# One fused transformer kernel: scan inputs with the next block's products beside them, and attention's key sets joined pair by pair

## Chip, core and metric

The kernel runs on one core of a Trainium2 chip. The metric is the device time in microseconds, the median of repeated runs of the whole program. The engines are named as in the profile: PE (TensorE), DVE (VectorE), ACT (ScalarE), POOL (GpSimd), SP (SyncE); their DMA queues are SPq, ACTq and POOLq.

## What is computed

The program computes two transformer blocks in a row on 512 tokens of width 1024. The first is a hybrid block (dilated window attention, a Mamba-2 scan, gates, SwiGLU); the second has two layers, the first with an RWKV-7 scan in both directions and a spatial gate, the second with an mLSTM. The change touches the attention of the first block and the inputs of the RWKV-7 scan for x in the second.

```python
DILATED_GROUPS = ((128, 1), (512, 4), (2048, 16))    # 3 groups x 8 heads of 64
# attention: each group by itself, with a bias by distance, then a softmax over the groups
logits = einsum(qb, kw) * HEAD_DIM ** -0.5 + bias     # bias (8, 128, 256) per group
m = max(logits); p = exp(logits - m); den = sum(p)
o = einsum(p, vw) / den;  lse = m + log(den)
alpha = softmax(stack(lses)); attn = sum(alpha * o)   # the join
merged = gates[:, :, 0] * (attn @ w_attn_branch) + gates[:, :, 1] * (ssm @ w_ssm_branch)
...
# scan inputs (rwkv_prep), for the context (256 tokens) and for x (512 tokens)
r, k, v = split(dwconv1d(p[..., o:o + 3 * B_WIDTH], b_shift), 3)
logw = -softplus(-(b_w0 + einsum(tanh(wd), b_w_up))) - 0.5;  decay = exp(-exp(logw))
a = sigmoid(b_a0 + einsum(ad, b_a_up))
kk = k * b_kk;  kk = kk * rsqrt(max(sum(kk * kk), 1e-12))
k_dir = k * (1 + (a - 1) * b_ka)
```

## The kernel before

Each float32 matmul against a weight is made of three: `wload` loads 512 KB of weights (`wraw`, by SPq), ACT rounds it to a high part (`whi`, L292), DVE takes the rest (`wlo`, L293), and `mm3` or `tok` issue low x high, high x low and high x high (L301 to L303, L384 to L386). The three tiles have three buffers each. One unit of 512 KB stands for 24 matmuls of 128x512 (L301 to L303 with 8 blocks of rows, or 4 token tiles with 2).

The order of the work is written by hand with generators: `par` takes one step of each in turn, `merge` runs that to the end, and `blend` and `between` hand out steps by a count of matmul columns (`self.work`). A scheduler then lays the instructions out at compile time on each engine, by this order and by when it expects operands and buffers; on the chip every engine and queue works through its list in order.

**Attention.** `rel_bias` makes the bias tables. For each group a matmul gives an 8-partition row table (one per head, 384 or 256 wide), a DVE copy brings it to SBUF, and a POOL DMA writes it to DRAM (`scr`) 128 times in a row; a second POOL DMA reads that back with a row pitch one element shorter, which shifts the row for each partition (`B0`, `B12`). POOL's queue holds these five DMAs in order, and the read of a table stands before the write of the next but one. Meanwhile V is projected (12 units of `w_v`). Then four head pairs `hp` follow: `units` (products, DVE maximum, ACT Exp, transposes, products with V) runs in step with `qk` of the next pair, for the last pair with 5 of 8 gate products (`gates`). There are two key sets: `sid` 0 is group 0, `sid` 1 is groups 1 and 2. Each has its maximum and its denominator in `st` and its output in `Os`.

`attn_join` joins the two sets of all heads at once, when all pairs are done: transpose `st`, write to DRAM (`dstat`), read back with the heads on 8 partitions (`R`), weights by maximum, Exp, sums and reciprocal (8x512 each), write (`dw`), read back on all partitions (`Wb`, 2 DMAs for each pair), and per pair two multiplies, an add and the split to `ah`, `al`. All these DMAs are SP's. The rest of the gates runs beside it. Behind it 8 products with `w_ab` (4 units) read `ah`, `al`.

**Scan inputs.** `mix0_proj` runs three products (blocks 16 to 18), then four blocks `b`. Each block has three products (`block_mm`, r, k, v, 24 matmuls each, a step ends after three rows of blocks), each evacuated by `conv3` in one ACT and two DVE operations; then a chain on DVE, ACT and POOL with six small products (sum of squares L1346; per direction decay L1357 and rate L1362; the bonus L1402 behind the whole chain) and the DMAs that store the scan's inputs. Every product there, and the chain's, takes one of the two PSUM buffers of `psO` (`fps`). It runs for the context (T = 256) beside the first block's FFN, and for x (T = 512, `two` = 2: r, k, v and four chain tiles have two buffers) beside the first steps of the scan itself (`mix0_scan`, L1480 to L1626), with products of `ada_units` (L1017) in between.

Of the kernel before, what the change touches and what calls it, by code (L numbers as in the profile page):

```python
# [249 lines left out]
class Kern:  # L250
# [177 lines left out]
    def rel_bias(self, pool):  # L428
# [6 lines left out]
        tab, es = flat()[:NBUCKET + 1, :896], flat()[:8]  # L435
# [3 lines left out]
        nc.gpsimd.dma_start(lhs[0:NBUCKET], D["relb"])  # L439
        off = 0  # L440
        for g, L in enumerate((384, 256, 256)):
            ps = self.btile()[:8, :L]
            nc.tensor.matmul(ps, lhs[:, g * 8:(g + 1) * 8], tab[:, off:off + L], start=True, stop=True)
            e = es[:, off:off + L]
            off += L
            nc.vector.tensor_copy(e, ps)
            scr = self.dram.tile([8, P * L + 512], F32, name="scr%d" % g)
            dst = scr[:, :P * L].rearrange("h (p l) -> h p l", l=L)
            nc.gpsimd.dma_start(dst, e.unsqueeze(1).to_broadcast([8, P, L]))
            src = scr[:, :P * (L - 1)].rearrange("h (p l) -> p h l", l=L - 1)  # L450
            if g == 0:
                nc.gpsimd.dma_start(B0, src[:, :, 0:256])
            else:
                nc.gpsimd.dma_start(B12[:, :, (g - 1) * P:g * P], src[:, :, 0:P])
        return B0, B12

    def attn_unit(self, pool, hp, sid, half, qT, kT, V, bias, st, O):
# [9 lines left out]
        for u in range(2):  # L467
# [13 lines left out]
            for e in range(2):  # L481
                h = 2 * hp + e
                nc.vector.tensor_tensor_reduce(p[:, e, u, lo:], S[e][:, u, lo:], bias[:, h, lo:], 1.0, -3e38,
                                               op0=ALU.add, op1=ALU.max, accum_out=st[:, 2 * sid, h, i:i + 1])
        mx = st[:, 2 * sid, 2 * hp:2 * hp + 2, 2 * half:2 * half + 2]
        nc.vector.tensor_scalar(ng.rearrange("p (e u) -> p e u", e=2), mx, -1.0, None, op0=ALU.mult)
        for u in range(2):
            i = 2 * half + u
            lo = P if sid == 0 and i == 0 else 0
            for e in range(2):  # L490
                h = 2 * hp + e
                nc.scalar.activation(p[:, e, u, lo:], p[:, e, u, lo:], AF.Exp, bias=ng[:, 2 * e + u:2 * e + u + 1],
                                     accum_out=st[:, 2 * sid + 1, h, i:i + 1])
# [24 lines left out]
    def attention(self, xT, ah, al, other):  # L518
# [3 lines left out]
        with self.tc.tile_pool(name="ao", bufs=1) as op:  # L522
          st = op.tile([P, 4, 8, 4], F32, name="st")
          Os = op.tile([P, 4, 2, SEQ], F32, name="Os")
          with self.tc.tile_pool(name="at", bufs=2) as pool:
# [26 lines left out]
            def units(hp, qT, kT):  # L552

                last = None
                for sid in range(2):
                    O = self.psO.tile([P, SEQ], F32, name="pso")
                    for half in range(2):
                        u = self.attn_unit(pool, hp, sid, half, qT, kT, V, (B0, B12)[sid], st, O)
# [12 lines left out]
            for hp in range(4):  # L571
                merge(units(hp, *qk_[hp]), qk(hp + 1, *qk_[hp + 1]) if hp < 3 else islice(other, 5))
          with self.tc.tile_pool(name="ac", bufs=2) as pool:
              merge(self.attn_join(pool, st, Os, ah, al), other)

    def attn_end(self, last, Os):
        _, hp, sid, half, O = last
        if half:
            self.nc.scalar.copy(Os[:, hp, sid], O)

    def attn_join(self, pool, st, Os, ah, al):

        nc = self.nc
        ps = self.btile()[:, :P]
        nc.tensor.transpose(ps, st.rearrange("p a b c -> p (a b c)"), self.ident)
        sT = pool.tile([P, P], F32, name="sT", bufs=1)
        nc.vector.tensor_copy(sT, ps)
        dst = self.dram.tile([4, 8, 4, P], F32, name="dstat")
        nc.sync.dma_start(dst.rearrange("a b c p -> (a b c) p"), sT)
        R = pool.tile([8, 4, SEQ], F32, name="R", bufs=1)  # L590
        nc.sync.dma_start(R, dst.rearrange("a b c p -> b a (c p)"))
        v = lambda i: R[:, i].rearrange("h (r i) -> h i r", r=4)
        n = lambda t: t.rearrange("h (i r) -> h i r", r=4)
        W = pool.tile([8, 2, SEQ], F32, name="W", bufs=1)
        tm = pool.tile([8, 2, SEQ], F32, name="tm", bufs=1)
        M, L = tm[:, 0], tm[:, 1]
        V_, S_ = nc.vector, nc.scalar
        yield
        V_.tensor_tensor(n(M), n(R[:, 0]), v(2), op=ALU.max)
        V_.tensor_tensor(W[:, 0], R[:, 0], M, op=ALU.subtract)  # L600
        V_.tensor_tensor(n(W[:, 1]), v(2), n(M), op=ALU.subtract)
        S_.activation(W, W, AF.Exp)
        V_.tensor_tensor(L, W[:, 0], R[:, 1], op=ALU.mult)
        V_.tensor_tensor(n(M), n(W[:, 1]), v(3), op=ALU.mult)
        V_.tensor_tensor(L, L, M, op=ALU.add)
        V_.reciprocal(L, L)
        V_.tensor_tensor(W, W, L.unsqueeze(1).to_broadcast([8, 2, SEQ]), op=ALU.mult)
        dw = self.dram.tile([8, 2, SEQ], F32, name="dw")
        nc.sync.dma_start(dw, W)
        yield  # L610
        for hp in range(4):
            Wb = pool.tile([P, 2, SEQ], F32, name="Wb")
            for e in range(2):
                nc.sync.dma_start(Wb[64 * e:64 * e + 64], dw[2 * hp + e].unsqueeze(0).to_broadcast([64, 2, SEQ]))
            y = pool.tile([P, SEQ], F32, name="ay")
            z = pool.tile([P, SEQ], F32, name="az")
            V_.tensor_tensor(y, Os[:, hp, 0], Wb[:, 0], op=ALU.mult)
            V_.tensor_tensor(n(z), Os[:, hp, 1].rearrange("d (r i) -> d i r", r=4), n(Wb[:, 1]), op=ALU.mult)
            V_.tensor_tensor(y, y, z, op=ALU.add)
            self.dump("attnT%d" % hp, y)  # L620
            self.split(ah[:, hp], al[:, hp], y)
            yield
# [229 lines left out]
    def block1_(self, keep, c1):  # L852
# [5 lines left out]
        with tc.tile_pool(name="b1", bufs=1) as pl:  # L858
# [13 lines left out]
            with tc.tile_pool(name="ahl", bufs=1) as ap_:  # L872
# [3 lines left out]
                with tc.tile_pool(name="gp", bufs=1) as gp:  # L876
                    gts = [gp.tile([P, SEQ], F32, name="g%d" % i) for i in range(8)]
                    self.attention(xT, ah, al, self.gates(xT, 0, gts))
                    for s in range(4):
                        w = self.wload(D["w_ab"], s, 1)  # L880
                        for j in range(2):
                            fb = 2 * s + j
                            ps = self.ptile()
                            self.feat(ps, w, 0, (ah, al), kbn=4, off=j * 512)
# [424 lines left out]
    def mix0_proj(self, pool, T, xT, up, io):  # L1309
# [20 lines left out]
        for b in range(4):  # L1330
            rkv = []
# [917 lines left out]
```

## Time and profile before

| | |
|---|---|
| runs | 3446.86, 3434.73, 3446.99 us; median 3446.86 |
| profiled execution, own time | 3435.72 us |
| its span | 3433.8 us, so 1.9 us lie around it |
| PE, DVE, ACT, POOL busy | 93%, 59%, 40%, 7% of the span |
| mean granted clock | 0.972 |

A span is the time from the first to the last instruction of the profiled execution. [...] Matmuls overlap in the pipeline, so the time from one start to the next is the price of one, not its listed duration.

### The profile page before, as it was taken

How to read it: one execution, taken by the hardware profiler on the slowest of the kernel's cores; microseconds unless marked ns; L12 is line 12 of the kernel's file. 1: busy time of each engine (PE TensorE's matmuls, PEld its weight loads, DVE VectorE, ACT ScalarE, POOL GpSimd, SP SyncE). 2: the span in 40 equal slices, each digit the busy share in tenths (PEclk: the TensorE clock that was granted, in tenths of full speed). 3: DMA queues.
4: the chain of work that ended last, by engine and by line, in shares of the span. 5: the costliest groups of instructions: out<-in, count | busy, mean ns of one | idle time of the engine just before them, and what ended most of it. 6: DMA issues, size and time to landing. Idle time of an engine off the chain costs nothing.

```text
span 3433.8 us, 53206 instructions
## 1 busy us (share of the span) xinstructions
PE 3209.5 (93%) x21803; PEld 2567.3 (75%) x21803; DVE 2010.4 (59%) x3226; ACT 1383.1 (40%) x2294; POOL 226.9 (7%) x260
## 2 busy tenths in 40 slices
PE   6999799999889999889899999989999989899998
PEld 5877577777677788766577888767788767778887
DVE  2333567775645543556655656667565754766656
ACT  2233244342344442443344444446532444543323
POOL 0000000000100000022121121000000200000001
PEclk9999999999999999999899999999999989999999
DMA  7411343445444432434555544542322325232323
GB/s 135 128 62 62 109 140 128 135 148 177 148 138 136 128 111 98 139 119 119 151 164 164 169 160 137 177 168 89 108 95 92 133 95 172 89 105 92 98 92 111
DMA packets 216843, 430.96 MB, mean 126 GB/s; under 512 B 75426, under 2 KB 114546, under 8 KB 216344
## 3 DMA queue, kind: packets, MB, share of 16 engines
q1 hardware_dynamic: 193736, 370.09, 34.1%
q10 hardware_dynamic: 20464, 51.58, 4.0%
q0 software_dynamic: 2400, 5.90, 1.7%
q8 instruction: 171, 2.80, 0.3%
q14 instruction: 72, 0.59, 0.1%
HBM read 380.70 MB, written 46.79 MB: 124 GB/s over the span
## 4 chain that ended last, share of the span: by engine, by line
PE 77%; DVE 9%; DMA 7%; ACT 4%; issue 2%; POOL 0%; SPq 0%; ACTq 0%; POOLq 0%; DVEq 0%
PE psa L301 11%; PE psa L303 11%; PE psa L302 11%; PE psa L385 5%; PE psa L384 5%; PE psa L386 5%; PE pso L301 3%; PE pso L303 3%; PE pso L302 3%; DVE wlo L293 2%; DMA wraw<-in_w_v_dram 1%; PE psa L1552 1%; ACT whi L292 1%; PE psa L1562 1%; PE pso L1017 1%
## 5 line engine op out<-in xcount | busy, mean ns | idle before, releaser
L293 DVE TENSOR_TENSOR wlo<-wraw,whi 128x1024 fp32r<-128x1024 f32 x480 | 597.5, 1246 | 524.2 <-ACT whi L292 518.7
L292 ACT CAST whi<-wraw 128x1024 fp32r<-128x1024 f32 x482 | 503.7, 1046 | 773.0 <-PE psa L386 224.6
L301 PE MATMUL psa<-xh,wlo 128*128 128x512 f32 (+1 forms) x1760 | 693.3, 396 | 18.0 <-DVE wlo L293 10.7
L303 PE MATMUL psa<-xh,whi 128*128 128x512 f32 (+1 forms) x1760 | 684.7, 390 | 0.0
L302 PE MATMUL psa<-xl,whi 128*128 128x512 f32 (+1 forms) x1760 | 683.7, 389 | 0.0
L301 PEld LDWEIGHTS psa<-xh,wlo 128*128 128x128 f32 x1760 | 335.6, 192 | 97.6 <-DVE wlo L293 14.9
L303 PEld LDWEIGHTS psa<-xh,whi 128*128 128x128 f32 x1760 | 336.0, 191 | 72.7 <-issue 4.2
L302 PEld LDWEIGHTS psa<-xl,whi 128*128 128x128 f32 x1760 | 336.3, 191 | 71.6 <-issue 3.8
L1138 DVE SCALAR_TENSOR_TENSOR fc<-psa,f_cv,fc 128x441 f32<-128x441 f32 (+2 forms) x352 | 243.4, 692 | 41.4 <-ACT fc L1127 34.5
L301 PE MATMUL pso<-xh,wlo 128*128 128x256 f32 (+1 forms) x720 | 232.0, 322 | 0.6 <-ACT u L1445 0.5
L302 PE MATMUL pso<-xl,whi 128*128 128x256 f32 (+1 forms) x720 | 222.0, 308 | 1.0 <-DVE xl L347 1.0
L303 PE MATMUL pso<-xh,whi 128*128 128x256 f32 (+1 forms) x720 | 221.8, 308 | 0.0
L385 PE MATMUL psa<-wlo,ah 128*128 128x512 f32 x528 | 210.9, 399 | 2.8 <-DVE wlo L293 2.5
L384 PE MATMUL psa<-whi,al 128*128 128x512 f32 x528 | 209.0, 399 | 3.4 <-ACT whi L292 3.4
L386 PE MATMUL psa<-whi,ah 128*128 128x512 f32 x528 | 209.7, 398 | 0.0
L301 PEld LDWEIGHTS pso<-xh,wlo 128*128 128x128 f32 x720 | 137.0, 190 | 12.9 <-issue 1.7
L302 PEld LDWEIGHTS pso<-xl,whi 128*128 128x128 f32 x720 | 136.9, 190 | 9.6 <-DVE xl L347 1.6
L303 PEld LDWEIGHTS pso<-xh,whi 128*128 128x128 f32 x720 | 136.5, 190 | 8.2 <-issue 0.8
L384 PE MATMUL psa<-whi,xl 128*128 128x512 f32 x288 | 117.6, 410 | 19.3 <-ACT whi L292 16.0
L385 PEld LDWEIGHTS psa<-wlo,ah 128*128 128x128 f32 x528 | 99.0, 188 | 30.1 <-DVE wlo L293 6.3
L384 PEld LDWEIGHTS psa<-whi,al 128*128 128x128 f32 x528 | 98.8, 187 | 29.6 <-ACT whi L292 4.7
L385 PE MATMUL psa<-wlo,xh 128*128 128x512 f32 x288 | 117.2, 407 | 1.1 <-DVE wlo L293 1.1
(554 smaller groups left out, 5168.5 us busy)
## 6 DMA issues: line engine op xcount, KB each, us to landing
wraw<-in_f_up_dram SPq DMA_DIRECT2D x132, 512.0 KB, 3.8
wraw<-in_ada_w_dram SPq DMA_DIRECT2D x96, 512.0 KB, 3.6
wraw<-in_f_dn_dram SPq DMA_DIRECT2D x66, 512.0 KB, 3.5
wraw<-in_w_fi_dram SPq DMA_DIRECT2D x44, 512.0 KB, 3.5
wraw<-in_ab_f_dram SPq DMA_DIRECT2D x38, 512.0 KB, 3.8
wraw<-in_w_qk_dram SPq DMA_DIRECT2D x24, 512.0 KB, 3.7
wraw<-in_w_xbc_dram SPq DMA_DIRECT2D x24, 512.0 KB, 4.7
wraw<-in_c_f_dram SPq DMA_DIRECT2D x24, 512.0 KB, 4.3
```

The source lines that it names most:

```text
L292: nc.scalar.copy(hi, raw)
L293: (eng or nc.vector).tensor_tensor(lo, raw, hi.bitcast(F32), op=ALU.subtract)
L301: mm(ps, wl, xh, start=start, stop=False)
L302: mm(ps, wh, xl, start=False, stop=False)
L303: mm(ps, wh, xh, start=False, stop=stop)
L384: mm(ps, sl, wh[:, c], start=first and k == 0, stop=False)
L385: mm(ps, sh, wl[:, c], start=False, stop=False)
L386: mm(ps, sh, wh[:, c], start=False, stop=last and k == kbn - 1)
L1017: nc.tensor.matmul(ps[o:o + 32], self.cs[:, 4 * h + j, 22 - 2 * i:54 - 2 * i], raw[:, j * 256:(j + 1) * 256], start=h == 0, stop=h == 1, t ...
L1138: V_.scalar_tensor_tensor(o, pv[:, r0 + dr:r1 + dr, c0 + dc:c1 + dc], cw(i), o, op0=ALU.mult, op1=ALU.add)
L1552: mm(ps[h, d, b], Al[h, d, b], Tm[h, d, b], start=True, stop=True, tile_position=(64 * e, 64 * e))
L1562: mm(ps[h, d, b], lt[h, d, b], rt[h, d, b], start=True, stop=True, tile_position=(64 * e, 64 * e))
```

## The change

1. `rel_bias`: the 24 columns of the bias table are repeated 16 times on the free side (`rep`), so that the matmul gives each head's row on 16 partitions, 128 in all. The DRAM write then takes 8 copies from each of 128 partitions, in place of 128 copies from each of 8.
2. Attention: `st` and `Os` are kept by pair. `attn_join` does one pair, as a generator of five steps; the join of a pair runs beside the next pair's units, that of the last beside the remaining gates, of which there are 4 in place of 3. R has the pair's two heads and four row groups on 8 partitions, so that its operations are 8x128. The DMAs move from SP to ACT (5 per pair, `dstat`) and POOL (R, `dw`, two `Wb`).
3. Products with `w_ab`: 4 outputs at a time, first with the rows of the first three pairs for all four, then with those of the last pair.
4. `mix0_proj`: `blocks` (the three products) and `chain` are split; for x, the chain of block b takes turns with the products of block b + 1. For the context the order stays.

```diff
@@ -432,21 +432,24 @@
         B12 = pool.tile([P, 8, 256], F32, name="B12", bufs=1)
 
         flat = lambda: pool.tile([P, 2, 2, 256], F32, name="p").rearrange("p a b c -> p (a b c)")
-        tab, es = flat()[:NBUCKET + 1, :896], flat()[:8]
+        tab, es = flat()[:NBUCKET + 1, :896], flat()
         nc.gpsimd.dma_start(tab, D["btab"])
         lhs = self.small.tile([NBUCKET + 1, 24], F32, name="lhs", bufs=1)
         nc.vector.memset(lhs[NBUCKET:NBUCKET + 1], 1.0)
         nc.gpsimd.dma_start(lhs[0:NBUCKET], D["relb"])
+
+        rep = pool.tile([NBUCKET + 1, 24, 16], F32, name="pT", bufs=3)
+        nc.vector.tensor_copy(rep, lhs.unsqueeze(2).to_broadcast([NBUCKET + 1, 24, 16]))
         off = 0
         for g, L in enumerate((384, 256, 256)):
-            ps = self.btile()[:8, :L]
-            nc.tensor.matmul(ps, lhs[:, g * 8:(g + 1) * 8], tab[:, off:off + L], start=True, stop=True)
+            ps = self.btile()[:, :L]
+            nc.tensor.matmul(ps, rep[:, g * 8:(g + 1) * 8].rearrange("k h r -> k (h r)"), tab[:, off:off + L], start=True, stop=True)
             e = es[:, off:off + L]
             off += L
             nc.vector.tensor_copy(e, ps)
-            scr = self.dram.tile([8, P * L + 512], F32, name="scr%d" % g)
-            dst = scr[:, :P * L].rearrange("h (p l) -> h p l", l=L)
-            nc.gpsimd.dma_start(dst, e.unsqueeze(1).to_broadcast([8, P, L]))
+            scr = self.dram.tile([8, P * L], F32, name="scr%d" % g)
+            dst = scr.rearrange("h (r q l) -> (h r) q l", q=8, l=L)
+            nc.gpsimd.dma_start(dst, e.unsqueeze(1).to_broadcast([P, 8, L]))
...
@@ -520,8 +523,8 @@
         nc, D = self.nc, self.D
         self.psS = self.psB
         with self.tc.tile_pool(name="ao", bufs=1) as op:
-          st = op.tile([P, 4, 8, 4], F32, name="st")
-          Os = op.tile([P, 4, 2, SEQ], F32, name="Os")
+          st = op.tile([P, 4, 4, 2, 4], F32, name="st")
+          join = iter(())
           with self.tc.tile_pool(name="at", bufs=2) as pool:
             V = pool.tile([P, 12, 512], F32, name="V", bufs=1)
             B0, B12 = self.rel_bias(pool)
@@ -549,13 +552,13 @@
                             nc.vector.tensor_copy(t, ps)
                         yield
 
-            def units(hp, qT, kT):
+            def units(hp, qT, kT, Os):
...
@@ -569,57 +572,64 @@
             qk_ = [([], []) for _ in range(4)]
             merge(qk(0, *qk_[0]))
             for hp in range(4):
-                merge(units(hp, *qk_[hp]), qk(hp + 1, *qk_[hp + 1]) if hp < 3 else islice(other, 5))
-          with self.tc.tile_pool(name="ac", bufs=2) as pool:
-              merge(self.attn_join(pool, st, Os, ah, al), other)
+                Os = op.tile([P, 2, SEQ], F32, name="Os", bufs=2)
+                merge(units(hp, *qk_[hp], Os), qk(hp + 1, *qk_[hp + 1]) if hp < 3 else islice(other, 4), join)
+                join = self.attn_join(op, hp, st[:, hp], Os, ah, al)
+          merge(join, other)
 
     def attn_end(self, last, Os):
         _, hp, sid, half, O = last
         if half:
-            self.nc.scalar.copy(Os[:, hp, sid], O)
-
-    def attn_join(self, pool, st, Os, ah, al):
+            self.nc.scalar.copy(Os[:, sid], O)
+
+    def attn_join(self, pool, hp, st, Os, ah, al):
+
 
         nc = self.nc
...
+        V_, S_, G_ = nc.vector, nc.scalar, nc.gpsimd
+        ps = self.btile()[:32, :P]
+        nc.tensor.transpose(ps, st.rearrange("p a e c -> p (a e c)"), self.ident)
+        sT = pool.tile([32, P], F32, name="sT")
+        S_.copy(sT, ps)
+
+        dst = self.dram.tile([4, 2, 4, P], F32, name="dstat%d" % hp)
+        S_.dma_start(dst[0:2].rearrange("a e c p -> (a e c) p"), sT[0:16])
+        for x in range(4):
+            S_.dma_start(dst[2 + x // 2, x % 2].rearrange("c (r i) -> r c i", r=4),
+                         sT[16 + 4 * x:20 + 4 * x].rearrange("r (c i) -> r c i", c=4))
+        yield
+        R = pool.tile([8, 4, P], F32, name="R")
+        G_.dma_start(R, dst.rearrange("a e c p -> (e c) a p"))
         v = lambda i: R[:, i].rearrange("h (r i) -> h i r", r=4)
         n = lambda t: t.rearrange("h (i r) -> h i r", r=4)
...
+        M = pool.tile([8, P], F32, name="M")
+        V_.tensor_tensor(n(M), n(R[:, 0]), v(2), op=ALU.max)
+        V_.tensor_tensor(R[:, 0], R[:, 0], M, op=ALU.subtract)
+        V_.tensor_tensor(v(2), v(2), n(M), op=ALU.subtract)
+        W = R.rearrange("h (s k) p -> h s k p", k=2)
+        S_.activation(W[:, :, 0], W[:, :, 0], AF.Exp)
         yield
...
+        V_.tensor_tensor(W[:, :, 1], W[:, :, 0], W[:, :, 1], op=ALU.mult)
+        V_.tensor_tensor(n(M), n(R[:, 1]), v(3), op=ALU.add)
+        V_.reciprocal(M, M)
+        V_.tensor_tensor(R[:, 0], R[:, 0], M, op=ALU.mult)
+        V_.tensor_tensor(v(2), v(2), n(M), op=ALU.mult)
+        dw = self.dram.tile([2, 2, 4, P], F32, name="dw%d" % hp)
+        G_.dma_start(dw.rearrange("s e c p -> (e c) s p"), W[:, :, 0])
         yield
...
+        Wb = pool.tile([P, 2, SEQ], F32, name="Wb")
+        for e in range(2):
+            G_.dma_start(Wb[64 * e:64 * e + 64], dw[:, e].rearrange("s c p -> s (c p)").unsqueeze(0).to_broadcast([64, 2, SEQ]))
+        yield
+        y, z = Os[:, 0], Os[:, 1]
+        V_.tensor_tensor(y, y, Wb[:, 0], op=ALU.mult)
+        zv = z.rearrange("d (r c i) -> d r c i", r=4, c=4)
+        V_.tensor_tensor(zv, zv, Wb[:, 1].rearrange("d (c r i) -> d r c i", r=4, c=4), op=ALU.mult)
+        yv = y.rearrange("d (i r) -> d i r", r=4)
+        V_.tensor_tensor(yv, yv, z.rearrange("d (r i) -> d i r", r=4), op=ALU.add)
+        self.dump("attnT%d" % hp, y)
+        self.split(ah[:, hp], al[:, hp], y)
+        yield
 
     def dt_stage(self, xT, pool, tmp):
 
@@ -876,12 +886,15 @@
                 with tc.tile_pool(name="gp", bufs=1) as gp:
                     gts = [gp.tile([P, SEQ], F32, name="g%d" % i) for i in range(8)]
                     self.attention(xT, ah, al, self.gates(xT, 0, gts))
-                    for s in range(4):
-                        w = self.wload(D["w_ab"], s, 1)
-                        for j in range(2):
-                            fb = 2 * s + j
-                            ps = self.ptile()
-                            self.feat(ps, w, 0, (ah, al), kbn=4, off=j * 512)
+                    for s in range(2):
+
+                        w = self.wload(D["w_ab"], 2 * s)
+                        pss = [self.ptile() for _ in range(4)]
+                        for j, ps in enumerate(pss):
+                            self.feat(ps, w, j // 2, (ah, al), kbn=3, off=j % 2 * 512, last=False)
+                        for j, ps in enumerate(pss):
+                            fb = 4 * s + j
+                            self.feat(ps, w, j // 2, (ah, al), kbn=1, kbx=3, off=j % 2 * 512 + 384, first=False)
                             V_.tensor_tensor(gts[fb], ps, gts[fb], op=ALU.mult)
                             nc.sync.dma_start(accd[fb], gts[fb])
             with tc.tile_pool(name="ss2", bufs=1) as sp2:
@@ -1327,15 +1340,18 @@
                 S_.activation(g, ps, AF.Tanh, scale=0.5)
                 V_.tensor_scalar(g, g, 0.5, 0.5, op0=ALU.mult, op1=ALU.add)
                 nc.scalar.dma_start(io["g"], g)
-        for b in range(4):
-            rkv = []
+
+        def blocks(b, rkv):
+
             for j in range(3):
                 r = new("rkv%d" % j, two)
                 ps = self.fps()[:, :T]
                 yield from self.block_mm(4 + 4 * j + b, xT, ps)
                 self.conv3(r, ps, lambda q, j=j: self.bsh[:, 4 * j + b, q:q + 1], None, T)
                 rkv.append(r)
-            r, k, v = rkv
+
+        def chain(b, r, k, v):
+
             nc.sync.dma_start(io["v"][:, :, b].rearrange("c p t -> p c t"), ch(v))
 
             kk = new("kk")
@@ -1404,6 +1420,14 @@
             V_.tensor_tensor(bn, ps, v, op=ALU.mult)
             nc.scalar.dma_start(io["bn"][b], bn)
             yield
+
+
+        rkv = [[] for _ in range(4)]
+        for b in range(4):
+            if b == 0 or two == 1:
+                yield from blocks(b, rkv[b])
+            nxt = blocks(b + 1, rkv[b + 1]) if two == 2 and b < 3 else ()
+            yield from par(chain(b, *rkv[b]), nxt)
 
     def sgate(self, pool, T, xT, io):
 
```

## Rows read from the trace of the kernel before

**Rows 1.** The page, first part: busy us, share of the span, instructions.
```profile
PE 3209.5 (93%) x21803; PEld 2567.3 (75%) x21803; DVE 2010.4 (59%) x3226; ACT 1383.1 (40%) x2294; POOL 226.9 (7%) x260
```

**Rows 2.** PE in order of time, around a gap at the start: start, us.
```profile
56.02 0.39 PE L384 MATMUL psa<-whi,xl 128*128 128x512 f32 x1
56.25 0.40 PE L385 MATMUL psa<-wlo,xh 128*128 128x512 f32 x1
...
72.87 0.82 PE L384 MATMUL psa<-whi,xl 128*128 128x512 f32 x1 [15.98 <-ACT whi L292]
...
75.17 0.63 PE L384 MATMUL psa<-whi,xl 128*128 128x512 f32 x1
75.59 0.63 PE L385 MATMUL psa<-wlo,xh 128*128 128x512 f32 x1
```

**Rows 3.** Busy time by stretch: length, PE, PEld, DVE, ACT, POOL, clock, DMA, GB/s.
```profile
55.00:85.00 30.00, 12.84 (x45) 10.93 (x44) 2.95 (x3) 3.15 (x3) 0.93 (x1) 0.72 0.85 125
110.00:120.00 10.00, 6.91 (x24) 5.38 (x23) 4.75 (x6) 2.09 (x2) 0.90 (x1) 0.83 0.69 222
160.00:355.00 195.00, 191.60 (x1075) 141.56 (x1075) 71.42 (x197) 78.48 (x188) 0.94 (x3) 1.00 0.18 61
365.00:395.00 30.00, 14.63 (x52) 9.99 (x52) 20.64 (x24) 4.69 (x7) 0.00 (x0) 0.77 0.38 106
1500.00:1546.00 46.00, 37.19 (x529) 27.66 (x524) 31.16 (x43) 20.62 (x33) 13.63 (x15) 0.95 0.43 124
1540.00:1552.00 12.00, 7.03 (x34) 4.84 (x30) 7.01 (x10) 1.75 (x4) 5.04 (x4) 0.57 0.50 111
1546.00:1595.00 49.00, 44.34 (x531) 32.47 (x530) 34.93 (x45) 19.39 (x28) 11.57 (x11) 0.95 0.45 122
1580.00:1600.00 20.00, 15.34 (x235) 12.40 (x235) 17.29 (x24) 7.59 (x13) 8.93 (x9) 0.91 0.61 142
1595.00:1644.00 49.00, 40.58 (x410) 29.06 (x408) 35.22 (x48) 19.87 (x30) 8.89 (x12) 0.82 0.40 108
1625.00:1651.00 26.00, 17.53 (x128) 11.54 (x127) 22.13 (x28) 10.66 (x16) 4.34 (x6) 0.61 0.50 121
```

**Rows 4.** DMA issues of the first 160 us: count, KB each, median us to landing.
```profile
scr<-p POOLq DMA_DIRECT2D x2, 1024.0 KB, 41.7
scr<-p POOLq DMA_DIRECT2D x1, 1536.0 KB, 55.0
B<-scr POOLq DMA_DIRECT2D x1, 1024.0 KB, 8.0
```

**Rows 5.** Waits of the first 160 us: us in total, times, longest us.
```profile
ACT whi L292 <- DMA wraw<-in_w_v_dram: 46.0, 5, 30.5
```

**Rows 6.** POOL in order of time, from the start to 130 us.
```profile
27.63 2.19 POOL L449 DMA_DIRECT2D scr<-p  x2 [24.56 <-DVE p L446]
```

**Rows 7.** DVE in order of time at the join's first multiply.
```profile
380.56 0.69 DVE L617 TENSOR_TENSOR ay<-Os,Wb 128x512 f32<-128x512 f32 x1 [6.45 <-DMA Wb<-dw]
```

**Rows 8.** The chain that ended last, 100 to 430 us: start, us, what.
```profile
373.00 1.79 DMA dw<-W
375.39 5.08 DMA Wb<-dw
```

**Rows 9.** DVE by line, 352 to 395 us: busy us, mean ns, idle before.
```profile
L618 DVE TENSOR_TENSOR az<-Os,Wb 128x512 f32<-128x512 f32 x4 | 4.2, 1058 | 0.0
...
L606 DVE RECIPROCAL tm<-tm 8x512 f32<-8x512 f32 x1 | 3.3, 3341 | 0.0
...
L605 DVE TENSOR_TENSOR tm<-tm 8x512 f32<-8x512 f32 x1 | 0.7, 672 | 0.0
```

**Rows 10.** ACT in order of time, 1548 to 1549 us: a DMA issue.
```profile
1548.35 0.33 ACTq L1405 DMA_DIRECT2D zb<-sq  x1
```

**Rows 11.** Waits of PE between 1500 and 1700 us: us in total, times, longest.
```profile
PE pso L1402 <- DVE kds L1400: 13.9, 4, 5.0
...
PE pso L1362 <- ACT ta L1364: 2.3, 1, 2.3
```

More of the change, by code (lines that the diff above doesn't have):

```diff
@@ L483, in attn_unit @@
                 nc.vector.tensor_tensor_reduce(p[:, e, u, lo:], S[e][:, u, lo:], bias[:, h, lo:], 1.0, -3e38,
-                                               op0=ALU.add, op1=ALU.max, accum_out=st[:, 2 * sid, h, i:i + 1])
-        mx = st[:, 2 * sid, 2 * hp:2 * hp + 2, 2 * half:2 * half + 2]
+                                               op0=ALU.add, op1=ALU.max, accum_out=st[:, 2 * sid, e, i:i + 1])
+        mx = st[:, 2 * sid, :, 2 * half:2 * half + 2]
         nc.vector.tensor_scalar(ng.rearrange("p (e u) -> p e u", e=2), mx, -1.0, None, op0=ALU.mult)
@@ L492, in attn_unit @@
                 nc.scalar.activation(p[:, e, u, lo:], p[:, e, u, lo:], AF.Exp, bias=ng[:, 2 * e + u:2 * e + u + 1],
-                                     accum_out=st[:, 2 * sid + 1, h, i:i + 1])
+                                     accum_out=st[:, 2 * sid + 1, e, i:i + 1])
         yield
@@ L557, in units @@
                     for half in range(2):
-                        u = self.attn_unit(pool, hp, sid, half, qT, kT, V, (B0, B12)[sid], st, O)
+                        u = self.attn_unit(pool, hp, sid, half, qT, kT, V, (B0, B12)[sid], st[:, hp], O)
                         next(u)
@@ L578, in attn_end @@
         if half:
-            self.nc.scalar.copy(Os[:, hp, sid], O)
-    def attn_join(self, pool, st, Os, ah, al):
+            self.nc.scalar.copy(Os[:, sid], O)
+    def attn_join(self, pool, hp, st, Os, ah, al):
         nc = self.nc
[L584 to L591, printed above, removed]
+        V_, S_, G_ = nc.vector, nc.scalar, nc.gpsimd
[11 more added lines that the diff above has]
+        G_.dma_start(R, dst.rearrange("a e c p -> (e c) a p"))
@@ L592, in attn_join @@
         v = lambda i: R[:, i].rearrange("h (r i) -> h i r", r=4)
         n = lambda t: t.rearrange("h (i r) -> h i r", r=4)
[L594 to L597, printed above, removed]
-        yield
-        V_.tensor_tensor(n(M), n(R[:, 0]), v(2), op=ALU.max)
-        V_.tensor_tensor(W[:, 0], R[:, 0], M, op=ALU.subtract)
-        V_.tensor_tensor(n(W[:, 1]), v(2), n(M), op=ALU.subtract)
@@ L602, in attn_join @@
[L602 to L609, printed above, removed]
-        yield
[L611 to L622, printed above, removed]
+        M = pool.tile([8, P], F32, name="M")
```

## The prediction

> **What bounds the kernel now.** I read the page's busy shares first, then PE's matmuls in order of time, then busy time and granted clock by stretch, and last the waits of the stretches that are not full. PE is busy for 93% of the span, DVE for 59% [rows 1]. At the full clock a 128x512 matmul is issued every 0.23 us; behind a gap, where the granted clock has fallen to 0.5, every 0.42 us for a while [rows 2, 3]. [...]
>
> What a gap costs I count as stretch length minus matmuls times 0.23 us, where all matmuls are of that shape; that holds the idle time and the slow matmuls at once.
> - Start: 55 to 85 us has 45 matmuls, worth 10.4 us, so 19.6 us are lost; 110 to 120 has 24, worth 5.5, so 4.5 are lost [rows 3]. Sum 24.1 us.
> - Join: 365 to 395 us has 52 matmuls, worth 12.0, so 18.0 us are lost [rows 3].
> - Scan inputs of x, three blocks with a block behind them, 1500 to 1644 us: idle 8.8 + 4.7 + 8.4 = 21.9 us. Shapes are mixed here, so the clock is counted apart: a mean of 0.57 over 12 us means 10 us at half speed, in which PE was busy some 6.5 us and lost half, 3.2; 0.91 over 20 us loses 1.8; 0.61 over 26 us means 20 us, busy 13.8, and loses 6.9. Together 11.9, in all 33.8 us [rows 3].
>
> **Part one: tables from all partitions.** The three bias tables are written to DRAM from 8 partitions, each row 128 times. These writes land 55.0 and 41.7 us after their issue for 1536 and 1024 KB; the table read of 1024 KB into 128 partitions with rows of the same 1 KB lands in 8.0 us [rows 4]. While they run, weights arrive late: casts waited 46.0 us on w_v loads [rows 5], and PE once for 16.0 us [rows 2]. The change keeps bytes, rows and the number of DMAs, and spreads the source over 128 partitions (a row goes out 8 times from each of 16). The write price is not in the trace: at worst as before, at best the 8 us per MB of the read, 12 us for the first table and 20 for the first two side by side. I take the lower end, because the read differs only in direction. Issued at 27.6 us [rows 6], two tables would be out near 50, before the gap begins at 56.9 [rows 2], and the third would be short enough for the weights loaded ahead. Added is one DVE copy of 33x384 (a 128x512 operation takes 0.69 [rows 7]), and three copies of 128 instead of 8 partitions; DVE is busy 3 of the 30 us of the gap [rows 3], which hides it. Without that cover it would cost under 1 us. I keep back 3 us for weights that still share the engines: **minus 21** (bounds 0 and 24).
>
> [...]
>
> **Part two: the join by pairs.** Before, one join for all heads starts behind the last pair's last product and ends with the multiplies of four pairs, one behind another; the DMAs dw and Wb, 1.79 and 5.08 us, lie in the chain [rows 8]. Meanwhile three gates' products run, 17 us, and then nothing. After, the joins of pairs 0 to 2 run beside the next pair's units, where PE is busy 191.6 of 195 us, DVE 71 and ACT 78 [rows 3]: each adds to DVE about 2.5 us of small operations (the eight of 512 columns took 0.67 to 3.34 us [rows 9], 9.8 in sum; a quarter of the columns) and 3.5 us of multiplies and split, which is moved, not new. DMAs: 5 issues per pair on ACT's queue, 0.33 us each [rows 10], 1.7 us; 4 on POOL's, which is idle there. SP loses the 11 of the old join, so the w_xbc loads behind them come a little earlier, worth 0 to 2 us, not counted.
>
> Only the last pair's join can stall PE. Its latency: issues 1.7, first write 1.8 like dw, small operations 3, multiplies 0.69 [rows 7] and two of 1.06 [rows 9] and a cast, which I set at the 0.69 too, 3.5, some 1.5 of handing over, and three DMAs from POOL (R, dw, Wb). Those cost 1.8 + 1.8 + 5.1 = 8.7 if as on SP [rows 8] and 24 if each takes the 8.0 of a table read [rows 4]: 20 to 35 us. Its cover: four gates, 4 x 24 x 0.23 = 22.1, and the new first part of w_ab (four banks, three pairs each), 36 x 0.23 = 8.3, so 30.4 us. Between 0 and 5 us stay open; I take 3, which also pays for one gate fewer beside the last pair's units. If a DVE operation on R or Wb comes up before its data, the weight splits and softmax reductions queued behind it wait, and then PE; weights are three buffers deep, so most of it is covered: 2 us for three pairs. 18 - 3 - 2: **minus 13** (bounds 0 and 18).
>
> **Part three: the next block's products beside this block's chain.** The work stays the same. Before, the chain's last product waited 13.9 us in four times on DVE's chain [rows 11], and the 72 matmuls of the next block's products stood behind it in program order. After, a chain step alternates with a third of a product, so there is PE work for each step. The last block's chain still has no products beside it: that loss stays. The bound is DVE: in the three cycles it is busy 31.2 + 34.9 + 35.2 = 101.3 us of 144, and PE's work at full clock is 144 - 33.8 = 110.2 [rows 3]. With no gap at all DVE would be 92% busy, with in-order chains through ACT and POOL; it will not fill that well. I take 82%, 124 us: **minus 20**. Bounds: 33.8, and 0 if the two PSUM buffers that chain and products share give it back (below).
>
> **Sum.** 3435.7 (the profiled execution's own time) - 21 - 13 - 20 = 3381.7. Of the times shown two lie at 3447 and one at 3434.7, so the profile is of the lower kind, 11 us under the median; not knowing which kind the median will be, I add 5: **3387 us**.
>
> **Rivals.**
> - *PSUM slots.* Chain and products share two buffers. A wait of PE for such a slot took 2.3 us [rows 11]. A chain takes six slots; if in three blocks all 18 wait that long, 41 us are paid for 33.8 won: 3435.7 - 34 + 7 = 3409, with the offset 3414. For it: a product holds its slot through 5.5 us of products and three evacuation steps. Against it: the old chain met this wait once.
> - *The writes stay slow.* If the row size or the DRAM side sets the rate, part one gives nothing: 3408. Against it: the 8.0 us read.
> - *Everything closes.* All gaps go: 3435.7 - 24 - 18 - 34 + 5 = 3365. Against it: DVE at 92%.
> - *Slower: DVE waits for POOL's DMAs.* Each pair has two places where DVE can stand for a DMA chain (R, then dw and Wb). If all eight wait 9 us, near the 8.0 of a table read, with PE behind, 72 us are lost beside 54 won, plus 18: 3435.7 + 18 + 5 = 3459. It decides from 7 us per wait on. Against it: only one wait of that kind shows, 6.45 us long and on a DVE with no other work [rows 7], and three weights are loaded ahead. [...]
>
> **Numbers.** Forecast 0.62 (its own range 3372 to 3402), slots 0.14, slow writes 0.09, all closes 0.09, slower 0.04, no visible change by several halves 0.02. The range takes in the second to fourth: 3362 to 3420. A change under 0.5%, 17 us, can't be told from none here. Faster 0.90, same 0.06 (the 0.02 and the upper ends of slots and slow writes), slower 0.04.
>
> **What would show it.** Tables: the scr writes land in 10 to 25 us, and 55 to 85 us has over 110 matmuls. Join: DVE and ACT operations of 8x128 lie between the units, and the first product of the fourth pair waits under 5 us. Scan inputs: in 1450 to 1640 us the granted clock stays at 1.00 except behind the last chain, and the waits of the chain's last product fall under 5 us. Wrong would be: writes still at 40 us; a wait of DVE for R or Wb over 6 us with PE idle behind it; waits of PE for the chain's slots over 15 us in sum.

## The result and the profile after

The changed kernel takes 3390.75 us (median of 4 runs, 3381.05 to 3394.77); the kernel before, beside it, 3445.33 (4 runs, 3434.73 to 3446.99). The ratio is 0.9844, 95% interval [0.9813, 0.9875]: 54.6 us less. The forecast was 3387, the range 3362 to 3420. The profiled execution took 3387.07 us, with a span of 3385.3 and a mean clock of 0.975.

Busy time on the page of the changed kernel, as in [rows 1]:
```profile
PE 3209.0 (95%) x21806; PEld 2570.5 (76%) x21806; DVE 2009.6 (59%) x3250; ACT 1383.1 (41%) x2301; POOL 234.3 (7%) x276
```
PE has the same work in a shorter span. Its stretches, as in [rows 3] (length, PE, PEld, DVE, ACT, POOL, clock, DMA, GB/s):
```profile
55.00:85.00 30.00, 30.00 (x129) 30.00 (x129) 8.72 (x9) 5.94 (x6) 0.00 (x0) 1.00 0.28 95
110.00:120.00 10.00, 10.00 (x46) 8.29 (x45) 3.17 (x3) 3.02 (x3) 0.00 (x0) 1.00 0.32 105
160.00:340.00 180.00, 177.77 (x1006) 132.96 (x1007) 82.92 (x210) 71.53 (x173) 10.47 (x19) 1.00 0.23 72
360.00:380.00 20.00, 14.17 (x53) 8.93 (x52) 9.23 (x12) 4.96 (x7) 0.00 (x0) 0.83 0.42 138
1440.00:1490.00 50.00, 49.79 (x706) 37.81 (x706) 26.57 (x38) 16.00 (x25) 14.32 (x14) 1.00 0.33 107
1490.00:1540.00 50.00, 46.09 (x474) 30.96 (x473) 38.88 (x48) 24.29 (x37) 11.29 (x12) 0.97 0.44 122
1540.00:1590.00 50.00, 48.23 (x633) 34.54 (x632) 39.63 (x57) 24.16 (x37) 11.76 (x15) 1.00 0.52 145
1590.00:1640.00 50.00, 38.65 (x374) 25.51 (x373) 38.28 (x51) 21.35 (x32) 10.93 (x13) 0.86 0.57 142
1481.00:1633.00 152.00, 135.88 (x1522) 93.81 (x1520) 117.23 (x154) 73.96 (x109) 36.73 (x42) 0.96 0.49 131
```
The gap at the start is gone: 129 matmuls where 45 stood. In the scan inputs one stretch stays thin, 1590 to 1640, with the last chain. A loss after the attention, now in 360 to 380, stays too. The last row holds nearly all of the four chains: the first one's first product starts at 1484.8 us, the last one's bonus product at 1635.1. DMA issues, as in [rows 4] (count, KB each, median us to landing):
```profile
scr<-p POOLq DMA_DIRECT2D x2, 1024.0 KB, 10.6
scr<-p POOLq DMA_DIRECT2D x1, 1536.0 KB, 7.3
B<-scr POOLq DMA_DIRECT2D x1, 1024.0 KB, 10.2
```
The 55.0 and 41.7 us of the old writes are now 7.3 and 10.6. PE in order of time around the fourth pair's first product, and at the first product of the stage behind `w_ab` (start, us; in brackets the idle time before):
```profile
348.27 0.51 PE L301 MATMUL psa<-ah,wlo 128*128 128x512 f32 x1 [0.29 <-ACT ah L317]
349.00 0.51 PE L302 MATMUL psa<-al,whi 128*128 128x512 f32 x1 [0.22 <-DVE al L318]
...
373.95 0.60 PE L301 MATMUL psa<-xh,MT 128*32 128x512 f32 x1 [5.83 <-DVE MT L318]
```
The join no longer stalls PE; 25 us on, PE waits 5.8 us where it waited 2.3 before. Waits of PE from 1440 to 1645 us, as in [rows 11], and of DVE from 160 to 400 us (us in total, times, longest):
```profile
PE psa L1576 <- POOL vs L1514: 6.2, 1, 6.2
PE pso L1418 <- DVE kds L1416: 4.6, 2, 3.9
PE pso L1362 <- ACT sq L1360: 3.4, 1, 3.4
...
PE pso L1418 <- DVE rkv L1268: 0.5, 1, 0.5
...
PE pso L301 <- DVE rkv L1268: 0.3, 1, 0.3
PE pso L301 <- DVE sq L1365: 0.2, 1, 0.2
```
```profile
DVE Os L625 <- DMA Wb<-dw: 18.3, 4, 5.6
```
The 13.9 us for the chain's last product are 4.6. The longest wait, 6.2 us, is that of a product of the scan for a POOL copy. DVE stands 18.3 us for `Wb`, with no PE idle behind it.

**Stage lengths.** Executions of one kernel differ by some 12 us, so a single profile against another tells little of the whole. Three stretches, cut out by their first and last instructions, are steadier. A: first to last copy of V. B: from there to the store of `lad`, behind join, `w_ab` and the stage after it. C: from the store of the gate (`zg`) to the last store of the spatial gate (`zu`), which holds the scan inputs of x. "Rest" is the span less the three. In us:

| kernel | A | B | C | rest |
|---|---|---|---|---|
| before | 72.7 | 315.3 | 321.5 | 2724.3 |
| after, two profiles | 48.2, 48.2 | 300.1, 299.9 | 304.5, 309.2 | 2732.5, 2725.6 |
| e1_tables | 48.3 | 311.3 | 319.8 | 2729.9 |
| e2_join | 76.1 | 303.5 | 319.0 | 2734.0 |
| e3_scan | 78.0 | 318.7 | 309.0 | 2728.4 |
| e4_wab_old | 48.3 | 300.2 | 306.9 | 2726.6 |
| e5_wab_half | 48.3 | 298.5 | 305.8 | 2735.8 |
| e6_join_sp | 48.3 | 296.9 | 305.5 | 2727.5 |
| e7_chain_psA | 48.3 | 300.0 | 296.1 | 2725.2 |
| e8_no_recip | 48.2 | 303.7 | 317.2 | 2728.2 |
| e9_tab32 | 48.3 | 301.0 | 306.2 | 2731.5 |
| e11_before_psA | 73.0 | 319.2 | 296.4 | 2734.6 |
| e12_all | 48.3 | 293.1 | 297.5 | 2726.4 |

The rest is the same work in all, and spans 2724 to 2736: that is the difference between executions. A stage changes clearly only where its part was changed. Without an edit its length still varies by a few us, most in B, which spans 311.3 to 319.2 with the old part and 299.9 to 303.7 with the new one. Each row but "after" is one profile.

### The profile page after: what moved, and what is told of

It is laid out like the page before. It is cut to its first block, busy times and chain, and to the rows that moved or that the text cites. A ratio compares the mean times of both kernels' runs of the same rounds, so it can differ in the third digit from the quotient of the medians.

```text
span 3385.3 us, 53289 instructions
## 1 busy us (share of the span) xinstructions
PE 3209.0 (95%) x21806; PEld 2570.5 (76%) x21806; DVE 2009.6 (59%) x3250; ACT 1383.1 (41%) x2301; POOL 234.3 (7%) x276
## 4 chain that ended last, share of the span: by engine, by line
PE 79%; DVE 8%; DMA 6%; ACT 4%; issue 2%; POOL 1%; SPq 0%; ACTq 0%; POOLq 0%; DVEq 0%
PE psa L301 12%; PE psa L303 11%; PE psa L302 11%; PE psa L385 6%; PE psa L384 6%; PE psa L386 6%; PE pso L301 3%; PE pso L302 2%; PE pso L303 2%; DVE wlo L293 2%; PE psa L1576 1%; PE psa L1586 1%; PE pso L384 1%; PE pso L1030 1%; PE pso L385 1%
## 5 line engine op out<-in xcount | busy, mean ns | idle before, releaser
L386 PEld LDWEIGHTS psa<-whi,ah 128*128 128x128 f32 x528 | 99.2, 188 | 23.2
```

The source lines that it names most:

```text
L386: mm(ps, sh, wh[:, c], start=False, stop=last and k == kbn - 1)
```

## The experiments

Ratios are to the kernel before, run beside each, with a 95% interval.

**Each part alone** (e1, e2, e3): the kernel before with one part of the change.

```text
e1: rel_bias of the changed kernel
e2: attn_unit, attention, attn_end, attn_join and the w_ab order of the changed kernel
e3: mix0_proj of the changed kernel
```


> The kernel before with only the tables written from all partitions. Theory (each part closes its own gap, and the three add up): minus 25 us, since the last copy of V stands at 89.9 us in the kernel after and at 115.2 in the one before; scr writes land in 7 to 11 us; 55 to 85 us is full. Rival (the time comes back before the join, because the stage behind is paced by the weights' loads): the copy of V comes 25 us earlier, but the end of the program moves by less than 15.

> The kernel before with only the join by pairs and the w_ab products in their new order. Theory: from the kernel after, the stretch from the last copy of V to the last store of the gates is 19.8 us shorter, and 4 to 5 of them are given back at the next stage, where the first small products wait for loads behind the stores: minus 15 us. Rival (the joins beside the units stall DVE, and PE with it, and the 19.8 come partly from the tables): less than minus 10.

> The kernel before with only the next block's products beside the chain. Theory: minus 16 us, as between the stores of the first and the last scan input in the two traces; granted clock 1.00 up to the last chain. Rival (the order of the scan stage depends on what came before, so the 16 are chance of one profile): below 10 or above 25.

Measured: tables 3409.35 us, 0.9907 [0.9889, 0.9924]; join 3428.72, 0.9965 [0.9953, 0.9977]; scan inputs 3426.55, 0.9963 [0.9949, 0.9976]. Beside 3443.02 that is 34, 14 and 16 us by the medians, and 32, 12 and 13 by the ratios, 57 in sum. Each part does something; the tables do most. The 25 us expected of e1 were 7 to 9 too few; the 15 and 16 of e2 and e3 are met within 3. The rival of e1 falls; those of e2 and e3 (under 10 us) are unlikely, but the intervals reach down to 8.

**The changed kernel again** (e10), beside its variants e5, e6 and e7.

> The changed kernel again, beside the variants of it that run with it. All theories: 50 to 58 us under the kernel before, a ratio of 0.983 to 0.985. The parts alone gave 32, 12 and 13 us, 57 in sum; if the parts help or hurt each other the whole lies off this sum by more than 5 us, and if they are independent within it.

3389.34 us (5 runs), 0.9836 [0.9815, 0.9856]: 55.5 less, within 2 us of the sum. So far as intervals of some 7 us to either side can tell, the parts are independent.

**The order of the w_ab products** (e4, e5). e4 has the order of before; e5 splits only the first four outputs.

```diff
-for s in range(2):
...
+for s in range(4):             # e4: all eight outputs; e5: range(2, 4), behind the first four
+    w = self.wload(D["w_ab"], s, 1)
+    for j in range(2):
+        fb = 2 * s + j
+        ps = self.ptile()
+        self.feat(ps, w, 0, (ah, al), kbn=4, off=j * 512)
...
```


> The kernel after, with the w_ab products in the order of the kernel before (one output after another, all four pairs' rows in each). Theory (the new order is cover for the last pair's join): the first product that needs the fourth pair waits some 8 us more, and the clock falls behind that; the stores spread again, so the 4 to 5 us lost at the next stage come back; in sum 3 to 8 us slower than the kernel after. Rival (four gates are cover enough): no wait over 2 us there, the stores spread, and it is 3 to 5 us faster than the kernel after.

> The changed kernel with only the first four outputs of w_ab split into three pairs and the fourth; the last four are made one after another as before the change, so their evacuations and stores are spread over the stage instead of coming in a burst. Theory: the new order is worth its cover of 3.6 us and loses it again by the burst, since the next stage's first product waited 5.8 us; then this keeps the cover and loses the burst: 2 to 5 us faster than the changed kernel, a ratio of 0.9985 or lower against it, and the wait at the next stage falls to 2 us. Rival: the next stage is bound by the load of its weights, which starts when the stage before is through, and the wait stays at 4 us or more: no difference.

e4: 3385.51 us, 0.9832 [0.9819, 0.9844]; B 300.2 as in the changed kernel: by this stretch neither 3 us slower nor 3 faster (whole runs can't tell so little). Its waits of PE from 330 to 400 us:
```profile
PE psa L301 <- ACT ah L317: 3.6, 1, 3.6
PE psa L301 <- issue: 2.0, 1, 2.0
```
3.6 + 2.0 stand against 0.5 + 5.8 in the changed kernel. The new order wins 3.1 us at the fourth pair, and loses 3.8 at the next stage: its last four outputs come and are stored in a burst (stores from 361.4 to 364.5 us), ACT stands 5.6 us for the stores before it can go on, and the next weights come late. That the burst is the reason is read from this order; ACT stands 4.4 us at the same place in e4 and e5 too, for something else. e5 keeps the first and loses the second: its waits there are 0.2 and 2.3. 3378.25 us, 0.9809 [0.9788, 0.983], B 298.5. The waits moved as the theory said; the time by B is 1.5 us in one profile, and the intervals of whole runs overlap, so its 2 to 5 us are not shown.

**The queue of the join's DMAs** (e6).

```diff
-S_.dma_start(dst[0:2]...); G_.dma_start(R, ...); G_.dma_start(dw...); G_.dma_start(Wb...)
+nc.sync.dma_start(...)        # all of them
```


> The changed kernel with all DMAs of the join on SP's queue instead of ACT's and POOL's. Theory: the move of the queues matters, since SP's queue holds the weight loads in order and a join DMA that waits for its operand stands ahead of them; each of the four joins then holds up loads for the latency of DVE's small operations, some 5 us in three places, and with three weights loaded ahead part of it is covered: 3 to 15 us slower than the changed kernel, with ACT's casts waiting for weights in the attention. Rival: the weights loaded ahead cover it all, and the transfers from SP land a little sooner than POOL's: within 2 us.

3380.19 us, 0.9808 [0.9793, 0.9823], against 0.9836 [0.9815, 0.9856]: not 3 to 15 us slower; the theory falls. B is 3 us shorter in its one profile, just outside the 299.9 to 303.7 of the kernels without an edit there, and DVE waits half as long:
```profile
DVE Os L625 <- DMA Wb<-dw: 8.9, 4, 3.5
```
So the move of these DMAs off SP's queue was not needed, and may cost a little.

**PSUM buffers of the chain** (e7, e11): the six small products of the chain, for x, take buffers of `psA` (four, which the scan uses too); the block products, and later the spatial gate, keep the two of `psO`. e7 does it in the changed kernel, e11 in the kernel before, with its written order.

```diff
+pt = self.ptile if two == 2 else self.fps
 ...
-ps = self.fps()[:, :T]        # sum of squares, 2 decays, 2 rates, bonus
+ps = pt()[:, :T]
```


> The changed kernel with the small products of the chain, for x, in PSUM buffers of the other pool, so that chain and block products no longer share two buffers. Theory: shared slots cost nearly nothing, since PE's waits that look like a slot sum to under 1 us between 1440 and 1645 us: within 2 us of the changed kernel. Rival: the two slots hold the products back through the order that the scheduler writes, which shows as no wait of PE for a slot but as chain steps that come late: 5 to 12 us faster, with the last store of the scan's inputs that much earlier.

> The kernel before with only the chain's small products for x in the other PSUM pool; the written order stays, a block's chain ahead of the next block's products. Theory: two things kept the next products behind the chain, the written order and the two buffers, and each alone keeps them there, except at the last chain, where the spatial gate's products now begin beside it: 5 to 10 us faster, a ratio near 0.998, with PE's waits for the bonus product still over 3 us each in three blocks. Rival: the buffers alone kept them there, and the scheduler moves the products up once they have buffers of their own: 18 to 25 us faster, a ratio of 0.993 to 0.995, which would mean that the change's new order was not needed.

e7: 3371.15 us (3368.41 to 3374.68), 0.9784 [0.9769, 0.9799], 18 us under the changed kernel beside it (3379.41 to 3394.25). e11: 3422.16, 0.9939 [0.9921, 0.9957], 19 us under the kernel before. In both the theory falls and the rival holds, for e7 even beyond its 5 to 12 us: C shows 10 of the 18, and where the others lie is not shown. C is 296.1 and 296.4: the buffers alone, in the old order, give all that buffers and new order give together. The bonus products of the chain and, below each, the first product of the spatial gate (count, ns min/median/max, first and last start), in the changed kernel, in e7 and in e11:
```profile
L1418 PE MATMUL pso<-kds,masks x8: 592/682/1192, 1517.0 to 1635.1; 128*128 128x512 f32 x8
...
L384 PE MATMUL pso<-whi,xl x32: 394/397/1415, 1635.2 to 1675.8; 128*128 128x512 f32 x32
```
```profile
L1420 PE MATMUL psa<-kds,masks x8: 592/644/1220, 1512.3 to 1624.8; 128*128 128x512 f32 x8
...
L384 PE MATMUL pso<-whi,xl x32: 393/397/795, 1599.3 to 1663.5; 128*128 128x512 f32 x32
```
```profile
L1403 PE MATMUL psa<-kds,masks x8: 592/686/697, 1550.3 to 1672.1; 128*128 128x512 f32 x8
...
L384 PE MATMUL pso<-whi,xl x32: 393/397/794, 1651.6 to 1710.6; 128*128 128x512 f32 x32
```
The spatial gate takes two `psO` buffers at a time. In the changed kernel it starts 0.1 us behind the very last bonus product; with buffers of its own, the chain leaves both free, and the gate starts 25.5 us (e7) or 20.5 us (e11) before that product. In e11 the four chains also move together: 121.6 us from the first bonus store to the last, against 143.9 before and 118.0 after. So the scheduler itself moves the next products up, once there are buffers for them. That the order came out better by chance is unlikely: three kernels with the buffers apart (e7, e11, e12) agree within 1.4 us in C. PE's 6.2 us for the POOL copy stand in all seven profiles that have the new order and shared buffers (after twice, e3, e4, e5, e6, e9), and in none of these three.

**Less work for DVE** (e8). For x the reciprocal of the norm is left out; a constant stands in its place.

```diff
-V_.reciprocal(sq, sq)
+V_.tensor_scalar(sq, sq, 0.0, 0.02, op0=ALU.mult, op1=ALU.add)   # for x only
```


> The changed kernel, for x without the reciprocal of the norm of kk: a multiply-add that gives a constant stands in its place, so DVE has one operation of 0.4 to 0.7 us for one of 3.35 us in each of four blocks, 11 us less work. Theory: DVE's chain sets the pace of this stage, being busy 117 of 152 us, or 77%: the stage gets 6 to 11 us shorter, 3379 to 3383 us in all. Rival: the pace is set by the buffers and the handing over between engines, and DVE has slack beside it: only the last chain, which stands alone, gets 2.8 us shorter, 1 to 4 us in all.

3393.46 us, 0.9854 [0.9834, 0.9874]; C 317.2, 10.5 us longer than the mean of the seven profiles with the new order and shared buffers (306.7: after twice, e3, e4, e5, e6, e9). Both theories miss. In the last chain, ACT's square and DVE's product of this kernel (start, us, idle before):
```profile
1615.59 0.63 ACT L1360 ACTIVATE sq<-kk 128x512 f32<-128x512 f32 x1 [3.63 <-DMA zb<-sq]
```
```profile
1630.12 0.69 DVE L1413 TENSOR_TENSOR ex<-ex,rkv 128x512 f32<-128x512 f32 x1 [4.21 <-POOL dc L1412]
```
The square waits for the store of the bonus before it, whose buffer `sq` it takes over; the product waits for a POOL copy that stands behind two copies of the scan on POOL. Another duration of one operation gave another order, and the last chain got stuck twice, for 7.8 us in sum. So 11 us less work on DVE bought nothing. As the order changed with it, e8 alone does not settle what DVE's load is worth; e7 and e11 do more, which do the same work on DVE as their bases and are shorter.

**Tables from 32 partitions** (e9).

```diff
-rep = ... [NBUCKET + 1, 24, 16]; dst = "h (r q l) -> (h r) q l", q=8;  source [128, 8, L]
+rep = ... [NBUCKET + 1, 24, 4];  dst = "h (r q l) -> (h r) q l", q=32; source [32, 32, L]
```


> The changed kernel with the bias tables written from 32 partitions, 32 copies of each, in place of 8 copies from each of 128. Bytes and row sizes stay. First theory: the number of source partitions sets the rate, each giving its own share; then four times the partitions of before give a quarter of 55 us, so the first table lands in some 14 us, the copies of V end 0 to 4 us later than in the changed kernel, and the time stays within 3 us of it. Second theory: what made the old write slow was the use of half of the engines only; then 32 partitions write as fast as 128, 7 to 8 us. Third: the writes are slow from anything under 128 partitions, 30 us or more; then the third table is late and 10 us or more are lost again.

3383.09 us, 0.9829 [0.9811, 0.9846], A 48.3: no time is lost. Its writes, and then the stretch of 34 to 38 us, in which tables are written (in the changed kernel the first is already being read back), of the kernel before, of e9 and of the changed kernel:
```profile
scr<-p POOLq DMA_DIRECT2D x2, 1024.0 KB, 12.9
scr<-p POOLq DMA_DIRECT2D x1, 1536.0 KB, 11.0
```
```profile
34.00:38.00 4.00, 4.00 (x20) 3.30 (x19) 1.23 (x1) 1.05 (x1) 0.00 (x0) 1.00 1.00 54
```
```profile
34.00:38.00 4.00, 4.00 (x19) 3.31 (x18) 1.23 (x1) 1.05 (x1) 0.00 (x0) 1.00 0.98 192
```
```profile
34.00:38.00 4.00, 4.00 (x19) 3.34 (x18) 1.23 (x1) 1.03 (x1) 0.92 (x1) 1.00 1.00 315
```
The 16 DMA engines are busy in all three (1.00, 0.98, 1.00), and move 54, 192 and 315 GB/s. Four times the partitions gave 3.6 times the rate, four times more again 1.6 times. The first theory is the nearest; the second, half of the engines, can't give more than a factor of 2, while the first write went from 55.0 to 11.0, and falls. One such write does take only about half of the engines' time. POOL's queue in the kernel before, from 60 to 70 us with two writes in flight, and from 101 to 109 with the third one alone (packets, MB, share of 16 engines):
```profile
q0 software_dynamic: 115, 0.50, 86.6%
```
```profile
q0 software_dynamic: 88, 0.36, 43.6%
```
Two writes take twice the engines' time and move 50 GB/s, where one moves 45: the engines did not set the rate. What did set it, beyond that it rose with the partitions, is not shown; the 54, 192 and 315 GB/s hold the weight loads of the stretch too, and the 315 a read-back.

**All variants together** (e12): e5, e6 and e7 in one.

> The changed kernel with three of its variants at once: the chain's small products for x in the other PSUM pool, the join's DMAs on SP's queue, and only half of w_ab in the new order. Theory: the chain's pool gave 18 us by the medians (8.5 of it before the last store of the scan's inputs), and the other two 9 and 11 us by the medians but only 3 and 1.4 us by their traces, so that most of their medians is the spread between executions; the sum by the traces is 13 to 23 us under the changed kernel, 3366 to 3376 us, a ratio of 0.977 to 0.980 to the kernel before. Rival: the medians hold as they stand and add up, 3350 us, a ratio of 0.973.

3366.93 us (3364.81 to 3372.63), 0.9783 [0.9766, 0.9799]. The theory holds. Against e7 alone, 0.9784, the two others add nothing that whole runs show, though B is 293.1. It beats both kernels, the changed one by 18 to 21 us by the ratios.

## Why the prediction was right

By the stages, as means over the profiles of kernels that have the old or the new part as the change has it: A 75.0 to 48.3, minus 26.7; B 316.1 to 301.4 (after twice, e2, e7, e8, e9), minus 14.7; C 320.1 to 306.7, minus 13.4. The sum is 54.8. Predicted were 21, 13 and 20, in sum 54. The sum is right because two mis-sized terms cancel: that part is luck.

- **Tables, minus 21: undersized by 6.** The mechanism was right, and the row taken for the price, the 8.0 us read, was a little dear: the first two writes were out after 12.5 us, not 20. The new writes land in 7.3, 12.5 and 8.7 us, where 10 to 25 were set as a sign. The 3 us kept back for late weights were not lost: 55 to 85 us is full, and 72.7 to 48.3 is 24.4, the 24.1 that were counted. And the profile of before is a mild case: A is 72.7 there and 73.0 to 78.0 in the other three kernels with the old tables. Half of the engines standing idle, the second theory of e9, would account for a factor of 2, not for 55.0 to 7.3. The share of 0.85 in that gap is that of two writes in flight; one alone took 43.6% of the engines' time.
- **Join, minus 13: right.** The first product of the fourth pair waited 0.5 us, not the 3 taken. What is not in the sum is the burst of stores behind the new `w_ab` order, some 3.5 us at the next stage. The cover of 8.3 us that the new order was counted for was worth 3.1. The 1.5 us of handing over in the latency was the author's estimate; no run shows it alone.
- **Slower by POOL's DMAs: fell**, by the reason given. DVE did stand for `Wb`, four times, 5.6 us at the longest, under the 7 from which it would decide; `R` cost no wait, and PE had work.
- **Scan inputs, minus 20: oversized by 7, and for a wrong reason.** The step that failed is "the bound is DVE", with its 82%. DVE was busy 117.2 of 152 us (77%), but e7, with the same work on DVE, needs 10 us less, and e8, with 11 us less work, is no faster. The buffers bind first: with them apart C falls by 23.4, near the 20 of the forecast, with or without the new order. From the first bonus store to the last it went from 143.9 to 118.0 us, more than the forecast 144 to 124; but the first comes 89.0 us behind the gate's store where it came 79.5, because the next block's products now stand beside its chain. One reading was off too: the 26 us from 1625 to 1651, from which 6.9 us of the gap were taken, reach 7 us past the three blocks.
- **PSUM slots: the rival was at work, and its sign was blind.** I set waits of PE for a slot of over 15 us as the sign; those seen sum to 1.0 us. But two buffers are a limit already when the order is written. A product that has no buffer is put behind the one that frees it, and in the trace that is no wait for a slot, but an empty PE ahead of the product before it. That "the last block's chain still has no products beside it: that loss stays" was taken for a fact of the work; it was the slots. The 10 us between 306.7 and 296.7 (the mean of e7, e11 and e12) are its price in C, some 8 of them ahead of the last bonus store. So far the rival was right; its price, 41 us of waits, was not.
- **Offset, plus 5.** The median of before beside the change was 9.6 over its profile, that of the change 3.7 over its own. "Rest" shows a part of it: 2724.3 in the profile of before is the lowest of all, 5 under the mean of 2729.3.
- **The clock.** The granted clock, TensorE's as a share of full speed, has two values in the traces of before and after, 1.00 and 0.50; before, it is at 0.50 for 192.9 us of the span, after for 166.8. The 10 and 20 us counted at half speed are there: 0.50 from 1541.0 to 1551.2 us and from 1629.9 to 1650.2. After, in 1440 to 1640 us, it fell behind the last chain (0.86), as said, and a little in 1490 to 1540 (0.97), behind the 3.4 us wait for ACT.

What remains open: why the join's DMAs on SP left DVE 9 us less of waiting, and how much of e5's and e6's lower medians is real. Not tested is another buffer of the chain: of its tiles only three (`ta`, `cs`, `ex`) have two buffers for x, and `sq`, which holds the square and later the bonus, has one. In the changed kernel ACT stood 11.4 us for the store of the first chain's bonus before it could begin the second chain's square, and PE 3.4 us behind that.

## What to carry to other kernels

A wait list shows no slot that the order was written around: where a stage is thin and its products stand right behind the user of the same few buffers, give one side other buffers before rewriting the order. The table writes from 8 partitions, two at a time, filled all engines (1.00 of 34 to 38 us) and moved 54 GB/s with the weight loads beside them, where 315 went at the same share in the changed kernel: read GB/s beside the busy share. To split a total into parts, cut the trace into stretches by fixed instructions: their lengths repeat to a few microseconds (8 at the worst here) when whole runs differ by twelve.

## What was not expected of the hardware

Two DVE products of the last chain took 1.75 us beside POOL's, against 0.69 alone. Operations of that chain in the changed kernel, DVE and then POOL (start, us):
```profile
1624.15 0.69 DVE L1395 TENSOR_TENSOR ta<-cs,ta 128x512 f32<-128x512 f32 x1
...
1629.90 1.75 DVE L1410 TENSOR_TENSOR ex<-ex,rkv 128x512 f32<-128x512 f32 x1
1631.57 1.75 DVE L1395 TENSOR_TENSOR ta<-cs,ta 128x512 f32<-128x512 f32 x1
```
```profile
1629.46 1.64 POOL L1414 TENSOR_TENSOR kds<-kds,l 128x512 f32<-128x512 f32 x1
1631.06 1.71 POOL L1563 TENSOR_TENSOR Al<-A,masks 128x512 f32<-128x512 f32 x1
```
The same operation (L1395) takes 0.69 us alone and 1.75 beside a POOL product, and L1410 ahead of it 1.75 too, twice in a row in the one chain that PE waits for: 2.1 us. At 1510.25 and 1511.95 us, beside the same two lines of POOL, L1410 and L1395 take 1.77 and 1.76. It is not so for every DVE product: `y<-psa,y` (L1247), at 2670.41 us, takes 0.68 beside a POOL product that runs from 2669.66 to 2671.64. What makes the difference is not shown.
